# A two-level Winograd matmul: other homes for some results, and a new order of preparatory work in its first three groups

## The chip, the cores and the metric

The kernel runs on one NeuronCore of a Trainium2 chip. The metric is the device time of one execution in microseconds (us), lower is better. A core has a matrix engine (PE), a vector engine (DVE), a scalar engine (ACT), a general engine (POOL), a queue processor (SP) which here issues nearly all transfers, and 16 DMA engines that carry them out. Each engine takes its instructions strictly in the order in which the program gave them, and waits on semaphores for the others.

## The reference

```python
def setup_inputs():
    B, S, D = 8, 2048, 2048
    return {"x": np.random.randn(B, S, D).astype(np.float32),
            "w": np.random.randn(D, D).astype(np.float32)}

def reference(x, w):
    cs = np.cumsum(x, axis=1)
    diff = cs - np.concatenate([np.zeros(...), cs[:, :-1, :]], axis=1)
    return np.matmul(diff, w).astype(np.float32)
```

The differences of a running sum are the terms themselves, so the result is x times w: 16384 rows of x, each of 2048 numbers, times a 2048 x 2048 matrix.

## The kernel before, in words

**Tiles of x.** The 16384 rows are cut into 128 tiles of 128 rows, here called tile 0 to tile 127. The first four are multiplied plainly in bf16 while w still arrives. The others go in groups of four, named by their first tile g: tiles g, g+1, h = g+2 and h+1. Group 4 is done by `group_plain`, groups 8, 12, 16 and so on, by `group`. The change touches the end of the plain part and groups 4, 8 and 12.

**Preparing a tile.** Five steps: `load` (two transfers of 512 KB), `weigh` (ACT sums the absolute values of each half, two instructions, line 112), `scale_of` (two tiny DVE instructions and one on POOL), `narrow` (ACT writes the scaled tile as f16, two instructions, line 143), `turn` (two transposes by DMA, line 156). All tiles share five buffers `F`, so a load has to wait for the tile that had its buffer. Tile 5 is the exception: it is loaded over `xP`, the plain part's turned x, once that part's rows 0 and 1 are done.

**First level.** Two tiles are one block row each of a 2 x 2 block scheme: tile g gives A11 and A12, tile g+1 gives A21 and A22 (halves of its 2048 numbers). w gives B11, B12, B21 and B22, each 1024 x 1024. In Winograd's form seven products take the place of eight, with S1 = A21+A22, S2 = S1-A11, S3 = A11-A21, S4 = A12-S2, and T1 = B12-B11, T2 = B22-T1, T3 = B22-B12, T4 = B21-T2. S1g is the S1 of tiles g and g+1, S1h that of h and h+1. DVE makes the S (`total`, one instruction each, line 502) and the T (`less`, line 499). One `product` on PE is 16 matmuls (8 steps of k, two halves n of 512 columns) into a pair of PSUM banks. In `group_plain` the four pairs are X (banks 0, 1), Y (2, 3), Z (4, 5) and V (6, 7).

**Second level.** In the groups from 8 on, some of the first-level products are themselves done by seven `quarter` products of four matmuls. The "rows" of this level are tiles g and h, and the quarters of w that it needs (`Inner`: Q1, Q2, Q3, Q4) are made once by `first` (Q1 and Q2), `fourth` (Q4) and `third` (Q3): `in_2` from B21, `in_3` from B22, `in_4` from T4, `in_5` from T1. Each of these is four DVE instructions of 128 x 512 (`first` has eight). `in_2`, `in_4` and `in_5` keep their Q4 in one tile, `flow`, which `keep_flow` copies out to memory (`spill`) and `bring_flow` copies back. In group 8 the order of quarters for A12 B21 on PE is: a11, s1, a12, s2, s4, then half of product S2g T2 (P6g), then s3, the other half of P6g, a22, and then the product S2h T2 (P6h) and a part of S3g T3 (P7g). The next seven are `seven(A3, in_3, ...)`, the last are those of T4 with `in_4`.

**Results.** A result tile C (128 x 512, f32) is begun by ACT from PSUM (`keep`, line 539), added to by DVE (`add`, line 542) and stored by SP (`put`, line 553). The seven tiles `c0` to `c6` go round: a tile that is stored goes to the end of the list `free`, and the next user waits until the store has landed. The results of the plain part go through five tiles `o` (`opool`), through spare tiles of the ring `wb`, and for one row through `F`. One 512-column piece of the plain part, `left_over`, is done as 16 matmuls into bank 2 and copied out by ACT.

**Order.** The order of work on each engine is the order of the program text: `after(...)` chains each instruction behind the one before on its engine. So what stands early in the text, stands ahead in an engine's queue, and an instruction that waits, holds all that is behind it.

Of the kernel before, what the change touches and what calls it, by code (L numbers as in the profile page):

```python
# [10 lines left out]
def kernel(  # L11
# [59 lines left out]
    def bank(i):  # L71
        return psum.tile([P, NB], f32, name=f"b{i}")
# [88 lines left out]
    with tc.tile_pool(name="ring", bufs=7) as ring, tc.tile_pool(  # L161
# [100 lines left out]
        def plain_out(h, r):  # L262
            for n in here(h, r):
                if h == r == 0:
                    c = F[:, 2, ds(n * NB, NB)]
                elif h == 0 or r > 0:
                    c = opool.tile([P, NB], f32, name="o")
                else:
                    c = ring.tile([P, NH], bf16, name="wb").bitcast(f32)
                after("act", lambda: nc.scalar.copy(c, ps[r][n]))  # L270
                done.append((c, ds(r * P, P), ds(h * NH + n * NB, NB)))
# [81 lines left out]
        def block(dst, a, h, k, engine):  # L353
            src = whole[k][:, a, h, :].rearrange("p (n c) -> p n c", c=NB)
            if engine == "dve":
                after(
                    "dve", lambda: nc.vector.tensor_scalar(dst[k], src, uinv, None, MUL)
                )
            else:
                after(  # L360
                    "act", lambda: nc.scalar.activation(dst[k], src, COPY, scale=uinv)  # L361
                )


        def finish_row(r):
            for ko in range(KO - KQ, KO):
                plain(1, r, ko)
            plain_out(1, r)


        def left_over(ps):
            for ko in range(KO):
                after(
                    "pe",
                    lambda: nc.tensor.matmul(
                        ps,
                        xP[:, PLAIN - 1, ko, :],
                        (B11, B21)[ko // KH][ko % KH][:, 1, :],
                        start=(ko == 0),
                        stop=(ko == KO - 1),  # L380
                    ),
                )
            c = opool.tile([P, NB], f32, name="o")
            after("act", lambda: nc.scalar.activation(c, ps, COPY, scale=uw))
            done.append((c, ds((PLAIN - 1) * P, P), ds(NB, NB)))

        for k in range(4):
            block(B11, 0, 0, k, "dve")
# [18 lines left out]
        finish_row(2)  # L407
        for k in range(4, KH):
            block(B21, 1, 0, k, "dve")
        finish_row(3)  # L410
        for k in range(KH):
            block(B12, 0, 1, k, "dve")
        left_over(bank(2))
        for c, rows, columns in done:
            after("sp", lambda: put(c, rows, columns, nc.sync))
        weigh(PLAIN + 1)
        scale_of(PLAIN + 1)
        narrow(PLAIN + 1)
        turn(PLAIN + 1)
        load(PLAIN + 3, 0)  # L420
        load(PLAIN + 3, 1)

# [26 lines left out]
    )  # L449
    inner = inpool.tile([P, 24, NB], f16, name="inner")  # L450
    flow = inpool.tile([P, 4, NB], f16, name="flow")
    spill = [spills.tile([P, 4, NB], f16, name=f"spill{i}") for i in range(4)]
    spare = [inner[:, j, :] for j in range(8, 24)]
    spare += [B12[k][:, n, :] for k in range(KH) for n in range(2)]
    spare += [B22[k][:, 0, :] for k in range(4, 8)]
# [1 line left out]
    S1 = [Part(inner[:, ds(2 * i, 2), :]) for i in range(2)]  # L457
    passing = [Quarter(inner[:, j, :]) for j in range(4, 8)]
    free = [cpool.tile([P, NB], f32, name=f"c{i}") for i in range(7)]

    def pair():
        return [one_c() for _ in range(2)]
# [26 lines left out]
    passed = [flow[:, k, :] for k in range(4)]  # L489

    def keep_flow(i):
        after("sp", lambda: nc.sync.dma_start(spill[i], flow))

    def bring_flow(i):
        after("sp", lambda: nc.sync.dma_start(flow, spill[i]))

    def less(dst, p, q):
        for k in range(len(dst)):
# [59 lines left out]
    def puts(c, t, h):  # L558
        for n in range(2):
            put(c[n], t, 2 * h + n)  # L560
# [26 lines left out]
    def group_plain(g, X, Y, Z, V):  # L587
        h = g + 2
        ug, uh, vg = unit[g], unit[h], unit[g + 1]
        A11g, A12g = parts(g)  # L590
        A11h, A12h = parts(h)
        A21g, A22g = parts(g + 1)
        A21h, A22h = parts(h + 1)
        S1g, S1h = S1
        S2g, S2h, S3g, S3h, S4g, S4h = A11g, A11h, A21g, A21h, A12g, A12h
        load(g + 4, 0)
        load(g + 4, 1)
        product(X, A11g, B11, True)
        for k in range(3):
            block(B22, 1, 1, k, "act")  # L600
        C11g = pair()
        keeps(C11g, X, ug)
        for k in range(3, KH):
            block(B22, 1, 1, k, "act" if k < 6 else "dve")
        product(V, A12g, B21, True)
        product(Y, A11h, B11, True)
        adds(C11g, V, ug)
        puts(C11g, g, 0)
        total(S1g, A21g, A22g, ADD)
        total(S3g, A11g, A21g, SUB)  # L610
        total(S2g, S1g, A11g, SUB)
        less(T2[:4], B22[:4], T1[:4])
        product(Z, A12h, B21, True)
        weigh(h + 1)
        C11h = pair()
        keeps(C11h, Y, uh)
        scale_of(h + 1)
        narrow(h + 1)
        turn(h + 1)
        load(h + 4, 0)  # L620
        less(T2[4:], B22[4:], T1[4:])
        vh = unit[h + 1]
        product(V, S1g, T1, True)
        C22 = pair()
        keeps(C22, V, vg)
        total(S4g, A12g, S2g, SUB)
        product(X, S2g, T2, False)
        C12g = pair()
        keeps(C12g, X, ug)
        less(T3, B22, B12)  # L630
        product(V, S4g, B22, False)
        weigh(g + 4)
        scale_of(g + 4)
        narrow(g + 4)
        load(h + 4, 1)
        turn(g + 4)
        load(g + 5, 0)
        load(g + 5, 1)
        product(X, S3g, T3, False)
        total(S1h, A21h, A22h, ADD)  # L640
        total(S3h, A11h, A21h, SUB)
        total(S2h, S1h, A11h, SUB)
        adds(C11h, Z, uh)
        puts(C11h, h, 0)
        adds(C12g, V, ug)
        puts(C12g, g, 1)
        product(Y, S2h, T2, False)
        C12h = pair()
        keeps(C12h, Y, uh)
        adds(C22, X, vg)  # L650
        puts(C22, g + 1, 1)
        total(S4h, A12h, S2h, SUB)
        product(Z, S1h, T1, True)
        weigh(h + 4)
        less(T4, B21, T2)
        scale_of(h + 4)
        C22 = pair()
        keeps(C22, Z, vh)
        narrow(h + 4)
        weigh(g + 5)  # L660
        product(Y, S3h, T3, False)
        in_2.first()
        in_2.fourth()
        load(h + 5, 0)
        load(h + 5, 1)
        keep_flow(0)
        scale_of(g + 5)
        adds(C22, Y, vh)
        puts(C22, h + 1, 1)
        product(Z, S4h, B22, False)  # L670
        in_2.third()
        adds(C12h, Z, uh)
        puts(C12h, h, 1)
        narrow(g + 5)
        turn(h + 4)
        product(X, A22g, T4, False)
        C21 = pair()
        keeps(C21, X, vg)
        puts(C21, g + 1, 0)
        turn(g + 5)  # L680
        load(g + 8, 0)
        load(g + 8, 1)
        in_3.first()
        in_3.fourth()
        in_3.third()
        product(Y, A22h, T4, False)
        C21 = pair()
        keeps(C21, Y, vh)
        puts(C21, h + 1, 0)
        weigh(h + 5)  # L690
        scale_of(h + 5)
        narrow(h + 5)
        turn(h + 5)


    def group(g, X, Y, q, e, v, w):
# [40 lines left out]
        load(next_k, 0)  # L737
        one()
        two()
        if g > PLAIN + 4:  # L740
            total(S1g, A21g, A22g, ADD)
            total(S3g, A11g, A21g, SUB)
            total(S2g, S1g, A11g, SUB)
# [22 lines left out]
        quarter(e, s4, Q.t22, False)  # L766
        add(C11g[1], e, ug)
        put(C11g[1], g, 1)
        total(S1h, A21h, A22h, ADD)
        total(S3h, A11h, A21h, SUB)  # L770
        scale_of(next_g)
        narrow(next_g)
        total(S2h, S1h, A11h, SUB)
        go(P6g, 2)
        quarter(q, s3, Q.Q3, False)
        add(C11h[1], q, uh)
        put(C11h[1], h, 1)
        weigh(next_h)
        load(next_k, 1)
        total(S4g, A12g, S2g, SUB)  # L780
# [105 lines left out]
            scale_of(next_l)  # L886
        else:
            if g == PLAIN + 4:
                in_4.first()
            one()  # L890
            two()
            weigh(next_k)
# [2 lines left out]
            turn(next_h, [0])  # L895
            scale_of(next_k)
            narrow(next_k)
            if g == PLAIN + 4:
                in_4.fourth()
                keep_flow(2)  # L900
                for k in range(4):
                    after("sp", lambda: nc.sync.dma_start(spill[3][:, k, :], in_3.t21[k]))
                in_4.third()
            else:
                in_5.first()
                in_5.fourth()
                keep_flow(1)
            product((v, w), S1g, T1, True)
            C22g = pair()
            keeps(C22g, (v, w), vg)  # L910
            adds(C12g, (v, w), ug)
            puts(C12g, g, 1)
            load(next_l, 0)
            product((q, e), S1h, T1, True)
            C22h = pair()
            keeps(C22h, (q, e), vh)
# [7 lines left out]
            turn(next_k, [0])  # L924
            adds(C22g, X, vg)
            puts(C22g, g + 1, 1)
            go(P7h, 4)
            adds(C22h, Y, vh)
            puts(C22h, h + 1, 1)
# [77 lines left out]
```

## Time and profile before

| what | value |
|---|---|
| time, three runs | 1500.28, 1501.83, 1503.62 us; median 1501.83 |
| the profiled execution, its own time | 1498.61 us |
| its span, first to last instruction | 1496.8 us |
| PE busy in the span | 1474.5 us (99%) |
| DVE busy | 1283.7 us (86%) |
| ACT busy | 914.4 us (61%) |
| share of the span on the chain that ended last, PE | 90% |
| granted clock of PE, mean | 0.998 |

All times below are in us from the start of the span of the profiled execution. A matmul of 128 x 512 is shown as 379 ns long, but a next one starts every 0.216 us (32 of them take 6.91 us on the chain), so a run of matmuls is shown 0.16 us longer than its share of PE. In an answer of the timeline, the columns are start, length, engine, line and operation, output and inputs, the count of instructions that are merged, and in brackets the idle time before them with what ended it.

### The profile page before, as it was taken

What the parts mean: (1) busy time and instruction counts of PE and PEld (TensorE: products, weight loads), DVE (VectorE), ACT (ScalarE), POOL (GpSimd) and SP (SyncE); (2) the same over time, 40 slices, a digit from 0 to 9 for tenths busy, and PEclk for the clock granted to TensorE, in tenths of its full rate; (3) what the DMA queues carried; (4) which work ended last, traced back from release to release, by engine and by line L of the source; (5) the groups of instructions that cost most, each with busy time, mean ns of one, the idle gap of its engine ahead of it and who ended that gap; (6) DMA issues with size and microseconds to landing.
All of it is one profiled execution on the core that took longest, in us unless ns stands there. A gap on an engine that the chain in (4) does not pass through costs nothing.

```text
span 1496.8 us, 21121 instructions
## 1 busy us (share of the span) xinstructions
PE 1474.5 (99%) x6799; PEld 663.8 (44%) x6799; DVE 1283.7 (86%) x2419; ACT 914.4 (61%) x1301; POOL 69.9 (5%) x136
## 2 busy tenths in 40 slices
PE   8988999999999999999999999999999999999998
PEld 3433444444444444444444444444444444444443
DVE  7987778888888888888888888888888888888887
ACT  5866566656666656666556657556656556666552
POOL 0200000000000000000000000000000000000000
PEclk9999999999999999999999999999999999999999
DMA  9988989999989999989998899999898999898983
GB/s 366 351 225 253 245 228 270 262 270 241 267 255 246 267 268 243 259 247 259 261 272 248 255 241 263 265 274 244 255 239 264 271 258 250 262 235 266 271 204 133
DMA packets 386975, 383.64 MB, mean 256 GB/s; under 512 B 275824, under 2 KB 276336, under 8 KB 386736
## 3 DMA queue, kind: packets, MB, share of 16 engines
q1 hardware_dynamic: 386304, 380.46, 91.9%
q0 software_dynamic: 560, 1.84, 0.3%
q8 instruction: 53, 0.87, 0.2%
q14 instruction: 58, 0.48, 0.1%
HBM read 180.88 MB, written 136.31 MB: 212 GB/s over the span
## 4 chain that ended last, share of the span: by engine, by line
PE 90%; DMA 4%; DVE 3%; ACT 2%; issue 1%; SPq 1%; DVEq 0%; ACTq 0%
PE b L531 46%; PE b L512 42%; PE b L250 2%; DVE c L542 2%; DMA W<-in_w_dram 2%; DMA x<-F 1%; DVE W L499 0%; ACT W L361 0%; ACT waste L112 0%; DMA W<-in_x_dram 0%; DMA out_dram<-c 0%; SPq L156 0%; DMA out_dram<-o 0%; DMA F<-in_x_dram 0%; ACT o L270 0%
## 5 line engine op out<-in xcount | busy, mean ns | idle before, releaser
L542 DVE SCALAR_TENSOR_TENSOR c<-b,u,c 128x512 f32<-128x512 f32 x1048 | 744.6, 746 | 164.3 <-PE b L531 92.1
L512 PE MATMUL b<-W,x 128*128 128x512 f16 x3072 | 717.1, 379 | 4.6 <-ACT c L539 2.6
L539 ACT ACTIVATE c<-b,u 128x512 f32<-128x512 f32 x496 | 316.9, 681 | 343.9 <-PE b L531 170.1
L512 PEld LDWEIGHTS <-x 128*128 128x128 f16 x3072 | 300.7, 98 | 369.0 <-issue 6.6
L143 ACT ACTIVATE F<-F,s 128x1024 f16<-128x1024 f32 x246 | 282.3, 1148 | 116.3 <-DVE s L131 112.0
L531 PE MATMUL b<-W,inner 128*128 128x512 f16 x1392 | 338.3, 379 | 0.0
L112 ACT ACTIVATE waste<-F 128x1024 uint8<-128x1024 f32 x246 | 259.6, 1055 | 91.4 <-DMA F<-in_x_dram 87.3
L531 PEld LDWEIGHTS <-inner 128*128 128x128 f16 x1744 | 170.6, 98 | 206.2 <-issue 0.5
L531 PEld LDWEIGHTS <-x 128*128 128x128 f16 x1560 | 152.5, 98 | 194.8 <-issue 15.4
L531 PE MATMUL b<-W,x 128*128 128x512 f16 x968 | 234.3, 379 | 1.4
L502 DVE TENSOR_TENSOR x<-x,x 128x1024 f16<-128x1024 f16 (+1 forms) x214 | 120.4, 574 | 6.5 <-PE b L512 1.1
L132 POOL TENSOR_SCALAR u<-m,uw 128x1 f32<-128x1 f32 x124 | 64.5, 525 | 1314.6 <-DVE m L129 1307.0
L531 PE MATMUL b<-flow,x 128*128 128x512 f16 x352 | 91.2, 382 | 3.1 <-DVE c L542 3.1
L502 DVE TENSOR_TENSOR inner<-x,x 128x1024 f16<-128x1024 f16 (+1 forms) x122 | 67.4, 553 | 3.8 <-DMA x<-F 3.8
L531 PE MATMUL b<-inner 128*128 128x512 f16 x240 | 61.6, 379 | 0.3 <-DVE c L542 0.3
L250 PE MATMUL b<-wb,xP 128*128 128x512 bf16 x240 | 57.4, 393 | 4.3 <-ACT wb L234 3.0
L531 PE MATMUL b<-inner,x 128*128 128x512 f16 x240 | 61.6, 379 | 0.0
L112 ACT ACTIVATION_READ_ACCUMULATOR waste<-F 128x1 f32 x246 | 46.7, 190 | 0.0
L502 DVE TENSOR_TENSOR x<-inner,x 128x1024 f16<-128x1024 f16 x62 | 42.3, 683 | 3.2
L502 DVE TENSOR_TENSOR inner<-inner 128x512 f16<-128x512 f16 x112 | 42.3, 419 | 1.0
L499 DVE TENSOR_TENSOR flow<-W,inner 128x512 f16<-128x512 f16 x120 | 42.6, 416 | 0.0
L237 DVE TENSOR_REDUCE wmax<-W 128x1 f32<-128x1024 f32 x32 | 39.0, 1219 | 3.0 <-DMA W<-in_w_dram 1.4
(54 smaller groups left out, 410.8 us busy)
## 6 DMA issues: line engine op xcount, KB each, us to landing
out_dram<-c SPq DMA_DIRECT2D x496, 256.0 KB, 4.0
F<-in_x_dram SPq DMA_DIRECT2D x246, 512.0 KB, 5.1
flow<-spill SPq DMA_DIRECT2D x57, 512.0 KB, 4.5
W<-in_w_dram SPq DMA_DIRECT2D x32, 512.0 KB, 9.7
W<-in_x_dram SPq DMA_DIRECT2D x16, 256.0 KB, 7.1
x<-F SPq DMA_TRANSPOSE x246, 4.0
out_dram<-o SPq DMA_DIRECT2D x7, 256.0 KB, 3.7
spill<-flow SPq DMA_DIRECT2D x3, 512.0 KB, 2.6
```

The lines of the kernel that those rows point to most:

```text
L112: lambda: nc.scalar.activation(waste, where[t][i], ABS, scale=1.0 / ROW, accum_out=sums_of[t][:, i : i + 1],),
L132: after("pool", lambda: nc.gpsimd.tensor_scalar(u, m, uw, None, MUL))
L143: lambda: nc.scalar.activation(narrowed(t)[:, ds(i * NH, NH)], where[t][i], COPY, scale=s),
L237: lambda: nc.vector.tensor_reduce(wmax[:, i : i + 1], wt, AX.X, MAX, apply_absolute_value=True),
L250: lambda: nc.tensor.matmul(ps[r][n], xP[:, r, ko, :], wb[h, ko][:, ds(n * NB, NB)], start=(ko == 0), stop=(ko == KO - 1),),
L499: after("dve", lambda: nc.vector.tensor_tensor(dst[k], p[k], q[k], SUB))
L502: after("dve", lambda: nc.vector.tensor_tensor(dst.all, p.all, q.all, op))
L512: said = nc.tensor.matmul(to[n], a[k], b[k][:, n, :], start=(first and k == 0), stop=(k == KH - 1), skip_group_check=True,)
L531: said = nc.tensor.matmul(to, a[k], b[k], start=(first and k == 0), stop=(k == 3), skip_group_check=True)
L539: after("act", lambda: nc.scalar.activation(c, p, COPY, scale=u))
L542: after("dve", lambda: nc.vector.scalar_tensor_tensor(c, p, u, c, MUL, ADD))
```

## The change

Eight edits, in the order of the program:

1. `plain_out`: of the plain part's second half, the first piece of row 1 goes to a ring tile and no longer to an `o` tile.
2. `left_over`: its result goes to a buffer of turned x (`turned_x[3][0]`, that of tile 7) in place of an `o` tile, and its store is issued with it; the whole call stands behind `weigh`, `scale_of`, `narrow` and `turn` of tile 5.
3. `weigh` of tile 5 stands ahead of the last row's matmuls and copies (`finish_row(3)`).
4. Group 4: the pair C11h lives in a part of `inner` which is not used until later (the home of `in_3`'s Q1), so the list `free` has two more to give; the list starts one further round.
5. The copies `spill0` and `spill3`, which nothing reads back, are gone: one transfer of 512 KB in group 4 and four of 128 KB in group 8.
6. Group 4's end: `weigh`, `scale_of`, `narrow` and `turn` of tile 11 stand ahead of the `keep` and `put` of the last pair C21; of `in_3`, only Q1 and Q2 are made there, the one ahead of `scale_of` of tile 11 and the other behind it. Its Q4 moves into group 8 behind the sums of x, and its Q3 to where `in_4.first` stood.
7. Group 8: S1h, S3h and S2h stand behind the addition of the quarter s3, and no longer ahead of it.
8. Groups 8 and 12: `first`, `fourth` and `third` of `in_4` (`first` and `fourth` of `in_5`) and the `keep_flow` are spread among and behind the additions of the products with T1.

```diff
@@ plain_out
-                elif h == 0 or r > 0:
+                elif h == 0 or r > 1 or r == 1 and n:
                     c = opool.tile([P, NB], f32, name="o")
                 else:
                     c = ring.tile([P, NH], bf16, name="wb").bitcast(f32)
@@ left_over
-            c = opool.tile([P, NB], f32, name="o")
+            c = turned_x[3][0].rearrange("p k m -> p (k m)").bitcast(f32)
             after("act", lambda: nc.scalar.activation(c, ps, COPY, scale=uw))
-            done.append((c, ds((PLAIN - 1) * P, P), ds(NB, NB)))
+            rows = ds((PLAIN - 1) * P, P)
+            after("sp", lambda: put(c, rows, ds(NB, NB), nc.sync))
...
+        weigh(PLAIN + 1)
         finish_row(3)
         for k in range(KH):
             block(B12, 0, 1, k, "dve")
-        left_over(bank(2))
         for c, rows, columns in done:
             after("sp", lambda: put(c, rows, columns, nc.sync))
-        weigh(PLAIN + 1)
         scale_of(PLAIN + 1)
         narrow(PLAIN + 1)
         turn(PLAIN + 1)
+        left_over(bank(2))
         load(PLAIN + 3, 0)
...
+    free.append(free.pop(0))
@@ group_plain
-        C11h = pair()
+        C11h = [inner[:, ds(j, 2), :].rearrange("p a n -> p (a n)").bitcast(f32) for j in (16, 18)]
         keeps(C11h, Y, uh)
...
         puts(C11h, h, 0)
+        del free[-2:]
...
-        keep_flow(0)
...
-        in_3.first()
-        in_3.fourth()
-        in_3.third()
         product(Y, A22h, T4, False)
+        weigh(h + 5)
+        less(in_3.Q1, in_3.t12, in_3.t11)
+        scale_of(h + 5)
+        narrow(h + 5)
+        less(in_3.Q2, in_3.t22, in_3.Q1)
+        turn(h + 5)
         C21 = pair()
         keeps(C21, Y, vh)
         puts(C21, h + 1, 0)
-        weigh(h + 5)
-        scale_of(h + 5)
-        narrow(h + 5)
-        turn(h + 5)
@@ group
         one()
         two()
+        if g == PLAIN + 4:
+            in_3.fourth()
...
-        total(S1h, A21h, A22h, ADD)
-        total(S3h, A11h, A21h, SUB)
+        if g > PLAIN + 4:
+            total(S1h, A21h, A22h, ADD)
+            total(S3h, A11h, A21h, SUB)
         scale_of(next_g)
         narrow(next_g)
-        total(S2h, S1h, A11h, SUB)
+        if g > PLAIN + 4:
+            total(S2h, S1h, A11h, SUB)
         go(P6g, 2)
         quarter(q, s3, Q.Q3, False)
         add(C11h[1], q, uh)
         put(C11h[1], h, 1)
+        if g == PLAIN + 4:
+            total(S1h, A21h, A22h, ADD)
+            total(S3h, A11h, A21h, SUB)
+            total(S2h, S1h, A11h, SUB)
...
             if g == PLAIN + 4:
-                in_4.first()
+                in_3.third()
...
-            if g == PLAIN + 4:
-                in_4.fourth()
-                keep_flow(2)
-                for k in range(4):
-                    after("sp", lambda: nc.sync.dma_start(spill[3][:, k, :], in_3.t21[k]))
-                in_4.third()
-            else:
-                in_5.first()
-                in_5.fourth()
-                keep_flow(1)
+            Q = in_4 if g == PLAIN + 4 else in_5
+            Q.first()
             product((v, w), S1g, T1, True)
...
             load(next_l, 0)
+            Q.fourth()
+            keep_flow(2 if g == PLAIN + 4 else 1)
             product((q, e), S1h, T1, True)
...
             puts(C22g, g + 1, 1)
+            if g == PLAIN + 4:
+                in_4.third()
             go(P7h, 4)
```

More of the change, by code (lines that the diff above doesn't have):

```diff
@@ L451 @@
     flow = inpool.tile([P, 4, NB], f16, name="flow")
-    spill = [spills.tile([P, 4, NB], f16, name=f"spill{i}") for i in range(4)]
+    spill = [spills.tile([P, 4, NB], f16, name=f"spill{i}") for i in range(1, 3)]
     spare = [inner[:, j, :] for j in range(8, 24)]
@@ L491, in keep_flow @@
     def keep_flow(i):
-        after("sp", lambda: nc.sync.dma_start(spill[i], flow))
+        after("sp", lambda: nc.sync.dma_start(spill[i - 1], flow))
     def bring_flow(i):
-        after("sp", lambda: nc.sync.dma_start(flow, spill[i]))
+        after("sp", lambda: nc.sync.dma_start(flow, spill[i - 1]))
     def less(dst, p, q):
```

## The prediction

> **What bounds the kernel now.** First the page: PE is busy for 99% of the span, so the ceiling on a gain from order alone is the 22 us in which it is not.
>
> ```profile
> span 1496.8 us, 21121 instructions
> PE 1474.5 (99%) x6799; PEld 663.8 (44%) x6799; DVE 1283.7 (86%) x2419; ACT 914.4 (61%) x1301; POOL 69.9 (5%) x136
> ```
>
> Then the windows, to see where PE idles (columns: stretch, length, busy us of PE, PEld, DVE, ACT, POOL, granted clock, DMA share, GB/s). From 270 on a group of 45 us loses nothing; the losses lie in the stretches that the change edits. In 140 to 160 the clock also falls.
>
> ```profile
> 80.00:100.00 20.00, 17.31 (x79) 7.66 (x79) 16.23 (x30) 19.17 (x26) 2.72 (x2) 1.00 0.70 209
> 110.00:120.00 10.00, 7.89 (x37) 3.48 (x36) 7.48 (x16) 5.06 (x9) 0.83 (x1) 1.00 0.89 328
> 140.00:150.00 10.00, 6.89 (x30) 2.76 (x28) 7.34 (x13) 4.61 (x7) 0.77 (x1) 0.94 1.03 265
> 150.00:160.00 10.00, 10.00 (x42) 4.26 (x41) 8.63 (x20) 8.85 (x14) 0.83 (x1) 0.89 1.05 287
> 315.00:360.00 45.00, 44.95 (x209) 20.29 (x208) 39.20 (x76) 27.73 (x40) 1.92 (x4) 1.00 0.92 255
> ```
>
> Last the timeline, for each loss with what ended it. Six waits of PE stand there, in brackets: 1.50, 1.85, 0.44, 2.11, 0.56 and 2.56.
>
> ```profile
> 80.40 10.09 PE L512 MATMUL b<-W,x 128*128 128x512 f16 x46 [1.50 <-ACT o L270]
> 92.34 3.61 PE L512 MATMUL b<-W,inner 128*128 128x512 f16 x16 [1.85 <-DVE inner L502]
> 99.89 10.67 PE L512 MATMUL b<-W,x 128*128 128x512 f16 x48 [0.44 <-ACT c L539]
> 116.34 13.97 PE L512 MATMUL b<-W,x 128*128 128x512 f16 x64 [2.11 <-ACT c L539]
> 141.88 1.90 PE L512 MATMUL b<-W,x 128*128 128x512 f16 x8 [0.56 <-DVE x L502]
> 148.92 1.87 PE L531 MATMUL b<-flow,x 128*128 128x512 f16 x4 [2.56 <-DVE c L542]
> 150.59 5.29 PE L512 MATMUL b<-W,x 128*128 128x512 f16 x20
> ```
>
> And what the engines behind these waits were themselves waiting for:
>
> ```profile
> 79.77 0.59 ACT L270 COPY o<-b 128x512 f32<-128x512 f32 x1 [5.62 <-DMA out_dram<-o]
> 83.52 0.21 DVE L129 TENSOR_SCALAR m<-m 128x1 f32<-128x1 f32 x1 [5.62 <-ACT waste L112]
> 115.60 0.69 ACT L539 ACTIVATE c<-b,u 128x512 f32<-128x512 f32 x1 [4.53 <-DMA out_dram<-c]
> 145.88 0.69 DVE L502 TENSOR_TENSOR inner<-x,x 128x1024 f16<-128x1024 f16 x1 [1.89 <-DMA x<-F]
> ```
>
> So there is no shortage of a resource: a copy waits for a store of its tile, all behind it on ACT waits too, and DVE sits on a sum of tile 11 with an addition behind it that PE wants.
>
> **Part by part.** PE's instructions, their count and order stay; only waits move. From X at 74.86 to the product after the first `seven(A3)` at 163.06, PE spends 88.2 us on 352 matmuls of 0.216, that is 76.0: 12.2 us are lost. The six waits are 9.0, 0.16 us each (1.0) for the overlap of a matmul's tail that a wait breaks, and the clock: the four matmuls at 148.92 take 1.87 where others take 1.02, the 20 behind them 5.29 where those at 197.63 take 4.48, together 1.66. The small rest stays.
>
> *Edits 1, 2 and 3, the plain part's end.* Now the last row needs no sixth `o` tile, so the copy at 79.77 loses its store. But the weighing of tile 5 (2.3 us on ACT) now stands ahead of that row's two copies (0.52 each). Its tile is loaded at 68.15 and takes 6.3 to land (the transfers' view), so 74.45. ACT is free at 73.65, weighs to 76.8, copies to 77.3 and 77.85. PE wants V's banks after X, at 74.86 + 16 x 0.216 = 78.3: the 1.50 goes, with 0.5 to spare; a load later by more than that costs its lateness.
>
> DVE's m of tile 5 comes when the blocks before it end, at 77.90, not 83.52; POOL's one instruction goes with it and nobody waits for it. Narrowing then runs 78.4 to 80.7, the left-over's copy 80.6 to 81.3. Its bank 2 is wanted by the third product Y at 81.8 (0.5 to spare; unhidden it costs up to 0.7). SP turns tile 5 at 79.5 to 82.1, stores the left-over (ready at 81.3, so no wait; 0.45 of issue) and loads tile 7 at 82.7, not 87.85. ACT's blocks of B22 start at 81.2, not 86.20: from here ACT and DVE are **5.0 earlier**. S1g ends at 87.0; its transposes (3.4 to land) are there at 84.3; PE wants it after 64 matmuls, at 88.7. The 1.85 goes. The keeps that end at 100.4 end at 95.4, and PE wants V again at 95.6: the 0.44 goes, with 0.2 to spare.
>
> *Edit 4.* C12h's second tile waited 4.53 for the store of C11h's first. With nine tiles it gets c1, stored long before: ACT keeps at 106.0 to 107.3, PE wants Y at 109.4, the 2.11 goes. Late next is C22h's second: it gets c5, C12g's first, whose store went out at 111.10 and now goes at 106.25; such stores took 5.5 to 5.9, so it lands about 111.9, the keep ends 112.5, and PE wants Z at 112.85. I cost it at nothing, at most 0.7. C11h's new home is written again at 121, ten us after its store.
>
> *Edit 5.* 512 KB leave at 123 (0.33 of SP), another 512 KB at 166 (2.25 of SP). PE waited for neither: nothing, and up to 2 us of DMA slack per piece at the page's 256 GB/s.
>
> *Edit 6.* PE now ends group 4 at 123.2 (130.14 before). Weighing, scaling and narrowing tile 11 runs on ACT from 121.1 to 126.15, and the two keeps of C21 (1.25) behind it end at 126.75 and 127.35. PE wants Y for group 8 at 126.65: **a new wait of 0.6**, from nothing (if the load of tile 11 were earlier still, which doesn't help: ACT is bound by tile 9's narrowing) to 1.3 (if the 0.7 above comes on top). Two stores on SP (1.7) wait behind the two transposes (2.7); the tiles have no taker for 10 us. In exchange tile 11's transposes go out at 129.45, right behind tile 12's loads. Those at 138.73 took 6.1; these have 512 KB of stores less ahead, so land by 137. Q4 of `in_3` (1.42 of DVE) falls into DVE's wait for the first quarter (128.0 to 131.6): nothing.
>
> *Edit 7.* The wait of 0.56 for S2g shrinks to 0.3, since C11h's keeps no longer come late. The addition that PE waited 2.56 for now has no transposes ahead of it: done at 138.65, wanted at 139.6. **2.56 and its tail go, and the clock's 1.66 with it.** Late next is S2h: three sums of 0.7 end at 140.7, PE wants it at 140.45: 0.3 new, and one us more for each us that tile 11 lands after 138.6.
>
> *The clock.* The idle rows of 1.50 to 2.11 left the clock at 1.00, that of 2.56 brought 0.89. The Trainium skill (TensorE: Matmul & The Clock Gate, Part 1) has the clock fall after an idle window of about 3.4 us, free-running, and warns of gaps above that; by this rule a gap of 2.56 would be harmless, the 1.66 not its price, and the gain 8.6. The row is taken.
>
> *Edit 8.* In group 8 DVE has 2.84 more to do than before (Q4 and Q3 of `in_3`, each 1.42, come over from group 4), but `in_3.third` replaces the 2.75 of `in_4.first` ahead of A3's sums, and stall and sums shift together: the seven start with the same lead of DVE (1.0) as now. Behind them T4's Q3 comes before C22h's additions, which end 0.8 later against PE; PE wants that bank 2 us later still. SP's `keep_flow` and its wait come behind two stores and a load, which gain 0.5. Nothing; bound -0.8 (group 16's two waits of 0.26 and 0.58 go too) to +0.8.
>
> **Sum.** Waits that go: 1.50 + 1.85 + 0.44 + 2.11 + 2.56 = 8.46; 0.26 of S2g's; five tails of 0.16 = 0.8; clock 1.66: 11.2. New: 0.6 + 0.3 = 0.9. Gain 10.3. Against the profiled execution 1498.61 this makes 1488.3; that one lay 3.2 below the median, so I forecast 1501.83 - 10.3 = **1491.5**.
>
> **Rivals.** *A: tile 11 stays late.* For it: DMA is at 1.03 of its share from 130 to 150, and group 16 still waits for transposes (0.80 and 0.96 on DVE). Against: it is issued 2 us earlier against PE. Then 2.56, its tail and the clock stay in another place (S2h): gain 10.3 - 4.4 = 5.9, 1495.9.
>
> *B: all small new waits vanish, and group 16's.* Gain 10.3 + 0.9 + 0.8 = 12.0: 1489.8.
>
> *C: no net change.* PE comes 10 us earlier to groups whose tiles are limited by DMA (0.92 to 1.05 of its share from 120 on), and gives the gain back in groups 8 to 16. Against: the steady groups run at the same share without a wait, the five us from 78 to 83 in which DMA moved almost nothing are filled, and 1 MB of stores is gone. 1501.8.
>
> *D, the other side: slower.* The same queue, worse: each of groups 8, 12 and 16 waits for a transposed tile at its first sums. A wait of w costs w + 0.16, and 1.66 of clock from 2.56 on. To be slower by 0.2% it has to eat 10.3 + 3.0, or 4.4 per group: w = 2.6 in each of the three is the point. The waits now are 1.89, 0.20 and 0.96. At w = 4 it costs 17.5 and ends at 1509.
>
> **How the numbers follow.** A change within 0.2%, 3.0 us, can't be told from none. My case 55%, A 18%, B 13%, C 6%, D 8%. My case, A and B are faster: 0.86; C same: 0.06; D slower: 0.08. My case's own range, with the bounds 0.7 and 0.7 and 0.8 up, 1.5 down, and a run-to-run spread of 1.7: 1488.5 to 1495. The range reaches to B below and A above with that spread: 1487.5 to 1498.5, which leaves out C and D.
>
> **What would show it.** Right: no bracket on the second product's wait for line 270; the vector engine's m of tile 5 near 78; no ACT wait on a store before Y's third use; tile 11's transposes ahead of C21's stores; no clock below 1.00 between 100 and 200; `seven` 10 us earlier, the steady groups 45.1 as before. Wrong: ACT idle before tile 5's weighing (load late); a bracket over 0.7 on PE for Z; DVE waiting for x<-F in group 8 by more than 1 us, or groups 12 and 16 longer than 46.3.

## The result, and the profile after

The changed kernel takes 1495.08 us (median of 12 runs, 1492.38 to 1498.42), the kernel before 1501.5 us in the same comparison (12 runs, 1498.82 to 1504.58). The ratio is 0.9959, with a 95% interval of 0.9948 to 0.9969: faster by 0.41%, some 6.2 us. The forecast was 1491.5 with 10.3 us of gain. The direction was right, the size too large by 4 us.

The profiled execution of the changed kernel took 1496.11 us, its span is 1494.3. Page, changed kernel:

```profile
span 1494.3 us, 21105 instructions
...
PE 1473.4 (99%) x6793; PEld 663.4 (44%) x6799; DVE 1283.9 (86%) x2419; ACT 913.6 (61%) x1301; POOL 69.4 (5%) x136
```

The engines' work is the same: the weight loads of PE and the instructions of DVE, ACT and POOL have the counts of before (six matmul records are missing from this trace). The timeline of PE, changed kernel, with every wait between the plain part's end and group 16 (columns as before; lines 512, 531, 539 and 542 of the kernel before are 514, 533, 541 and 544 here):

```profile
72.59 3.62 PE L375 MATMUL b<-W,xP 128*128 128x512 f16 x16
...
89.86 3.62 PE L514 MATMUL b<-W,inner 128*128 128x512 f16 x16
...
98.15 0.38 PE L514 MATMUL b<-W,x 128*128 128x512 f16 x1 [0.44 <-ACT c L541]
98.73 10.30 PE L514 MATMUL b<-W,x 128*128 128x512 f16 x47 [0.20 <-ACT c L541]
...
117.33 13.76 PE L514 MATMUL b<-W,x 128*128 128x512 f16 x63 [1.18 <-ACT c L541]
131.48 0.38 PE L514 MATMUL b<-W,x 128*128 128x512 f16 x1 [0.40 <-ACT c L541]
132.06 3.40 PE L514 MATMUL b<-W,x 128*128 128x512 f16 x15 [0.20 <-ACT c L541]
...
140.18 1.90 PE L514 MATMUL b<-W,x 128*128 128x512 f16 x8 [0.40 <-DVE x L504]
...
145.84 3.63 PE L514 MATMUL b<-W,x 128*128 128x512 f16 x16 [0.31 <-DVE x L504]
150.33 0.38 PE L514 MATMUL b<-W,x 128*128 128x512 f16 x1 [0.86 <-ACT c L541]
150.91 0.81 PE L514 MATMUL b<-W,x 128*128 128x512 f16 x3 [0.20 <-ACT c L541]
...
156.38 1.02 PE L533 MATMUL b<-W,x 128*128 128x512 f16 x4 [0.29 <-DVE c L544]
...
159.11 7.07 PE L514 MATMUL b<-W,inner 128*128 128x512 f16 x32
...
234.45 1.02 PE L533 MATMUL b<-inner 128*128 128x512 f16 x4 [1.11 <-DVE c L544]
241.38 1.02 PE L533 MATMUL b<-flow,x 128*128 128x512 f16 x4 [0.73 <-DVE c L544]
```

The large waits of before (1.50, 1.85, 2.11, 2.56) are gone, and nothing waits for line 270. In their place stand smaller ones, most of them on an ACT `keep`. What ACT itself waited for (timeline of ACT, changed kernel):

```profile
91.66 1.06 ACT L112 ACTIVATE waste<-F 128x1024 uint8<-128x1024 f32 x1 [1.94 <-DMA F<-in_x_dram]
116.59 0.69 ACT L541 ACTIVATE c<-b,u 128x512 f32<-128x512 f32 x1 [3.55 <-DMA out_dram<-c]
147.06 1.06 ACT L112 ACTIVATE waste<-F 128x1024 uint8<-128x1024 f32 x1 [2.08 <-DMA F<-in_x_dram]
```

Three transfers come too late: tile 7's load, the store of C12g's first tile, tile 14's load. Behind each of them a `keep` is queued whose PSUM bank PE wants. The windows of the changed kernel show the clock whole, and the steady group as it was (44.95 of 45 busy):

```profile
140.00:160.00 20.00, 18.16 (x81) 7.76 (x82) 15.13 (x31) 12.42 (x18) 1.11 (x2) 1.00 1.08 269
315.00:360.00 45.00, 44.95 (x209) 20.35 (x208) 39.20 (x76) 27.86 (x40) 1.92 (x4) 1.00 0.99 257
```

**One number for the stretch.** All of the change acts between the left-over's first matmul (line 375) and the product behind the first `seven(A3)` (the row of 32 matmuls, at 159.11 here). In between lie 368 matmuls, 79.5 us at 0.216. I call the time between these two rows the stretch: 162.89 - 71.41 = 91.48 before, 159.11 - 72.59 = 86.52 after. The two rows of the kernel before:

```profile
71.41 3.62 PE L375 MATMUL b<-W,xP 128*128 128x512 f16 x16
...
162.89 7.07 PE L512 MATMUL b<-W,inner 128*128 128x512 f16 x32
```

The stretch is read from each kernel's PE timeline, and leaves out the plain part, whose loads of w vary by a microsecond from run to run (line 375 starts between 70.92 and 72.75 in these profiles).

### The profile page after: what moved, and what is told of

Its sections match the earlier page's. It is cut to its first block, busy times and chain, and to the rows that moved or that the text cites. A ratio compares the mean times of both kernels' runs of the same rounds, so it can differ in the third digit from the quotient of the medians.

```text
span 1494.3 us, 21105 instructions
## 1 busy us (share of the span) xinstructions
PE 1473.4 (99%) x6793; PEld 663.4 (44%) x6799; DVE 1283.9 (86%) x2419; ACT 913.6 (61%) x1301; POOL 69.4 (5%) x136
## 3 DMA queue, kind: packets, MB, share of 16 engines
q0 software_dynamic: 560, 1.84, 0.3%
## 4 chain that ended last, share of the span: by engine, by line
PE 88%; DMA 5%; DVE 3%; ACT 2%; issue 1%; SPq 1%; DVEq 0%; ACTq 0%
PE b L533 45%; PE b L514 41%; DVE c L544 2%; PE b L250 2%; DMA W<-in_w_dram 2%; DMA F<-in_x_dram 2%; DMA x<-F 1%; DVE W L501 1%; ACT waste L112 0%; DMA W<-in_x_dram 0%; DMA out_dram<-wb 0%; ACT F L143 0%; SPq L156 0%; DVE x L504 0%; ACT wb L234 0%
## 5 line engine op out<-in xcount | busy, mean ns | idle before, releaser
L234 ACT CAST wb<-W 128x1024 bf16<-128x1024 f32 x32 | 32.2, 1059 | 15.6 <-DMA W<-in_w_dram 12.3
```

The source lines that it names most:

```text
L234: after("act", lambda: nc.scalar.copy(b, wt))
```

## The experiments

Two theories stood against each other. W: each wait has its own price, and the gain fell short because ACT runs into the three late transfers. D: the DMA engines are the bound in these groups, so PE gives back later whatever it wins. The column "stretch" is from one profile of each kernel (two of the kernel before and of the changed one). Each ratio is to the kernel before in the same comparison, and a difference between two rows of the table has an interval of about 0.0016 either way, 2.4 us: of the kernels built on the changed one, only the last two rows differ from it by more than that. For the others, the medians and the stretch have to be read together.

| kernel | median, us | ratio to before, 95% interval | stretch, us | group 16's waits |
|---|---|---|---|---|
| before (two profiles) | 1501.5 | | 91.48, 94.22 | 0.84, 1.00 |
| changed (two profiles) | 1495.08 | 0.9959 (0.9948 to 0.9969) | 86.52, 87.17 | 1.84, 2.13 |
| edits 1 to 3 alone | 1498.07 | 0.9977 (0.9967 to 0.9986) | 89.39 | 1.43 |
| edit 7 alone | 1500.33 | 0.9993 (0.9984 to 1.0002) | 92.37 | 1.19 |
| edit 4 alone | 1498.78 | 0.9978 (0.9969 to 0.9987) | 90.94 | 0.96 |
| changed, edit 7 undone | 1494.42 | 0.9951 (0.9939 to 0.9964) | 86.31 | 1.81 |
| changed, tile 11 behind again | 1494.77 | 0.9955 (0.9942 to 0.9969) | 85.81 | 2.29 |
| changed, tile 7's load early | 1495.85 | 0.9968 (0.9956 to 0.9981) | 85.57 | 1.98 |
| changed, home for C12g | 1492.95 | 0.9948 (0.9935 to 0.9960) | 83.79 | 2.78 |
| changed, tile 14's weighing behind | 1492.75 | 0.9945 (0.9932 to 0.9957) | 84.67 | 1.87 |
| these three together | 1491.48 | 0.9940 (0.9926 to 0.9954) | 82.56 | 1.63 |
| the last two of the three | 1492.59 | 0.9936 (0.9924 to 0.9949) | 82.05 | 1.45 |

### Edits 1 to 3 alone

The kernel before with the first three hunks of the change (`plain_out`, `left_over` and the place of tile 5's weighing).

> The kernel before with edits 1 to 3 alone (the plain part's end). Theory W (each wait has its own price; the changed kernel falls short of the forecast because ACT runs into three transfers that land too late: tile 7's load, the store of c5, tile 14's load): the waits of 1.50 and 1.85 go with their tails, the third (0.44) grows to some 1.7 us because tile 7's load lands after ACT wants it; gain about 2.5 us. C12h's store wait and the 2.56 with the fallen clock stay, at about the same size. Theory D (the DMA engines are the bound in these groups, so PE gives back later whatever it wins): PE starts group 8 earlier, but the waits in group 8 and at Y for C12h grow by as much; gain 0 to 1 us.

Measured: 0.9977, 3.2 us by the medians. PE's first two waits are gone, and the third, at V, is split in two as in the changed kernel (0.31 and 0.20): the 80 matmuls from 89.18 to 107.28 lost 0.8, where W had expected some 1.7. C12h's wait for its store stayed, and was larger than in the first profile of before: 3.63, with the clock down. W's gain of 2.5 lies in the interval (2.1 to 5.0 us); D's 0 to 1 doesn't. The wait in group 8 is 1.57 here, though, not 2.56.

### Edit 7 alone

```diff
-        total(S1h, A21h, A22h, ADD)
-        total(S3h, A11h, A21h, SUB)
+        if g > PLAIN + 4:
+            total(S1h, A21h, A22h, ADD)
+            total(S3h, A11h, A21h, SUB)
         scale_of(next_g)
         narrow(next_g)
-        total(S2h, S1h, A11h, SUB)
+        if g > PLAIN + 4:
+            total(S2h, S1h, A11h, SUB)
         go(P6g, 2)
         quarter(q, s3, Q.Q3, False)
         add(C11h[1], q, uh)
         put(C11h[1], h, 1)
+        if g == PLAIN + 4:
+            total(S1h, A21h, A22h, ADD)
+            total(S3h, A11h, A21h, SUB)
+            total(S2h, S1h, A11h, SUB)
```

> The kernel before with edit 7 alone (S1h, S3h, S2h of group 8 behind the addition). Theory W: the wait of 2.56 before the quarter a22 goes, the clock stays at 1.00 (1.66 more), and S2h, which still waits for tile 11's transposes that land near 145.8, holds the next product by about 0.9 us; gain 3 to 3.7 us. Theory D: the same transposes hold PE elsewhere for the same time; gain 0 to 1 us, and the clock falls all the same.

Measured: 0.9993, with an interval that holds 1, and 1.0 us by the medians. W's 3 to 3.7 is out. D's 0 to 1 holds, and the clock fell all the same, as D had said; but the place is not the one that D gave, as the timeline of PE for this kernel shows:

```profile
119.04 23.34 PE L512 MATMUL b<-W,x 128*128 128x512 f16 x95 [3.63 <-ACT c L539]
147.10 1.90 PE L512 MATMUL b<-W,x 128*128 128x512 f16 x8 [0.41 <-DVE x L502]
152.76 4.49 PE L512 MATMUL b<-W,x 128*128 128x512 f16 x20 [0.31 <-DVE x L502]
```

In its own place the edit does all that was forecast: the wait before the quarter a22 is gone, 0.31 before S2h's product remains, and the clock is at 1.00 there. But the wait at 119 is 3.63, not 2.11, and 95 matmuls took 23.34, of which 20.5 are their share at full clock. That wait lies ahead of the edit, in code that is the same as before. So it had to vary by itself, which the second profile of the kernel before was to tell.

### Edit 4 alone

```diff
+    free.append(free.pop(0))
...
-        C11h = pair()
+        C11h = [inner[:, ds(j, 2), :].rearrange("p a n -> p (a n)").bitcast(f32) for j in (16, 18)]
...
         puts(C11h, h, 0)
+        del free[-2:]
```

> The kernel before with edit 4 alone (C11h in inner, the list one round further). Theory W: the wait of 2.11 for C12h's second tile goes, and C22h's second, which now needs the store of C12g's first, is wanted near 118.4 while the store lands near 117, so no new wait; gain about 2.2 us, unless the 2.56 in group 8 grows with it, since tile 11's transposes are bound to the ACT chain. Theory D: gain 0 to 0.5 us, all given back at the wait for tile 11's transposes.

Measured: 0.9978, 2.5 us by the medians: W's 2.2 is met, D's 0 to 0.5 is not. The wait for C12h's tile is gone, but C22h's second tile came late as in the changed kernel (PE 0.88 at 120.75), which was not expected here. In the same profile PE waited 2.24 at 93.63, before the product of S1g, and the granted clock from 90 to 100 was 0.83; a wait of 2.24 again, at 149.65, left it at 1.00. Timeline of PE, this kernel:

```profile
93.63 5.30 PE L513 MATMUL b<-W,inner 128*128 128x512 f16 x16 [2.24 <-DMA F<-in_x_dram]
...
149.65 1.02 PE L532 MATMUL b<-flow,x 128*128 128x512 f16 x4 [2.24 <-DVE c L543]
```

### The kernel before, a second profile

No edit.

> The kernel before, unchanged, for a second profile. If the waits on a store vary from run to run: C12h's wait for its tile is anywhere from 4.5 to 6.5 us on ACT, PE's wait at Y 2.1 to 3.7, and where it is over 3 the clock falls there and not in group 8, whose wait is then about 1.6. If they don't vary: 2.1 and 2.56 again, with the clock at 0.89 from 150 to 160.

Timeline of PE, the kernel before, second profile:

```profile
80.26 10.09 PE L512 MATMUL b<-W,x 128*128 128x512 f16 x46 [1.84 <-ACT o L270]
92.54 3.61 PE L512 MATMUL b<-W,inner 128*128 128x512 f16 x16 [2.19 <-DVE inner L502]
118.23 22.35 PE L512 MATMUL b<-W,x 128*128 128x512 f16 x95 [3.79 <-ACT c L539]
151.72 1.02 PE L531 MATMUL b<-flow,x 128*128 128x512 f16 x4 [1.93 <-DVE c L542]
```

The waits on transfers do vary. The store of C11h's first tile took 6.70 from issue to landing in place of 5.39; ACT waited 6.21 for it in place of 4.53, and PE 3.79 in place of 2.11. The clock fell there, to 0.88 from 120 to 130, and in group 8 it was whole, with a wait of 1.93. So the profile on which the forecast's sum was made was a good one: its stretch was 2.7 us shorter than this one's. And the two waits go together: where the first was over 3.6 (here, and with edit 7 or edits 1 to 3 alone), the clock fell there, and the wait in group 8, where the code still had it, was 1.6 to 1.9. So edit 7 alone had a wait of 1.6 to 1.9 to take away, without a fall of the clock, and not the 4.4 of the first profile. The 1 us that it brought fits that; one profile of it can't show more.

### The changed kernel without edit 7

> The changed kernel with edit 7 undone (the sums S1h, S3h, S2h ahead of the addition again). Theory W: tile 11 is earlier in the changed kernel, so the quarter a22 waits for three sums, 0.7 to 1.5 us, without a fall of the clock; S2h's wait of 0.31 behind it goes; 0.5 to 1.2 us slower than the changed kernel, so 5 to 6 us faster than before. Rival: edit 7 carries most of the gain; the 2.56 and the fallen clock come back, and the kernel is 4 us slower than the changed one, 2 to 3 us faster than before.

Measured: 0.9951, against 0.9959 with the edit: no difference. Its stretch is 86.31. Timeline of PE, this kernel:

```profile
145.01 1.02 PE L533 MATMUL b<-flow,x 128*128 128x512 f16 x4 [1.40 <-DVE c L544]
```

Before the quarter a22 PE waits 1.40, because DVE waits 0.72 for tile 11's transposes, and the addition that PE wants stands behind the sums made from them. So with edit 6 and without edit 7 most of the wait is still there: with neither edit in this part it is 1.57 (edits 1 to 3 alone) and 2.24 (edit 4 alone). It costs nothing here, because in exchange the 0.31 before S2h's product and the 0.86 before P7g are gone (0.20 of the latter is left). Both theories had given it a cost.

### The changed kernel with tile 11 behind again

```diff
-        weigh(h + 5)
         less(in_3.Q1, in_3.t12, in_3.t11)
-        scale_of(h + 5)
-        narrow(h + 5)
         less(in_3.Q2, in_3.t22, in_3.Q1)
-        turn(h + 5)
         C21 = pair()
         keeps(C21, Y, vh)
         puts(C21, h + 1, 0)
+        weigh(h + 5)
+        scale_of(h + 5)
+        narrow(h + 5)
+        turn(h + 5)
```

> The changed kernel with one piece of edit 6 undone: weighing, scaling, narrowing and turning tile 11 stand behind the keeps and stores of the last C21 again; the rest of the change stays. Theory P (place decides: edit 6 brings tile 11 early enough that PE's 2.56 and the clock go even without edit 7): DVE's sum S1h waits 2 to 3 us for tile 11's transposes, PE waits 1.5 to 2.5 before the product of S2h (0.31 now), Y's 0.40 and 0.20 go; 0.5 to 2 us slower than the changed kernel. Rival (edit 7 alone cures that wait): no wait over 0.5 before the product of S2h, 0.5 us faster than the changed kernel.

Measured: 0.9955 and a stretch of 85.81, the same as with it. PE waits 0.78 before S2h's product in place of 0.31, and the 0.40 and 0.20 for C21h's keeps are gone. DVE waits 0.38 for tile 11, not 2 to 3. My expectation was wrong: tile 11's transposes, issued at 136.06 here, land early enough. So edit 7 cures the wait before a22 without this piece of edit 6. Of the two edits that I credited with the largest term, each can be taken out alone without a loss in time; what the changed kernel would take without both was not run.

### Tile 7's load early

```diff
+        load(PLAIN + 3, 0)
+        load(PLAIN + 3, 1)
         for c, rows, columns in done:
             after("sp", lambda: put(c, rows, columns, nc.sync))
...
         left_over(bank(2))
-        load(PLAIN + 3, 0)
-        load(PLAIN + 3, 1)
```

> The changed kernel, with tile 7's two loads issued ahead of the plain part's stores in place of behind the left-over's store. Theory W: tile 7 has landed when ACT wants to weigh it, ACT's waits of 1.94 and 0.19 go, and PE no longer waits for C22's keeps (0.44 and 0.20, some 1.7 us with what they hold up); 1 to 1.7 us faster than the changed kernel. Theory D: the same megabyte only moves, the stores and tile 8 come later for it, and the wait turns up at the next transfer (Z for C22h, or group 8); 0 to 0.4 us.

Measured: 0.9968, not faster than the changed kernel. In its place it worked: ACT no longer waits for tile 7, both brackets at V are gone, and the stretch is 0.95 to 1.6 us shorter than in the two profiles of the changed kernel. Tile 5's transposes went out 1.5 us later against the left-over (83.68 with line 375 at 72.75; 82.05 with 72.59), and DVE waited 1.42 for them: one megabyte ahead pushes back what stands behind, as D has it. PE shows no bracket there in this kernel, and group 16's waits are as large as before. So the profile has a gain that the five times don't show; whether it is lost further on or hidden in the spread, these runs don't tell.

### A home for C12g

```diff
-        C12g = pair()
+        C12g = [inner[:, ds(j, 2), :].rearrange("p a n -> p (a n)").bitcast(f32) for j in (20, 22)]
...
         puts(C12g, g, 1)
+        del free[-2:]
```

> The changed kernel, with the pair C12g also in a part of inner that is unused until the end of group 4 (the home of in_3's Q2), so no result waits for a store in group 4. Theory W: ACT's wait of 3.55 for the store goes, and PE's 1.18 at Z with it (about 1.5 us with its tail); narrowing tiles 10, 9 and 11 comes some 3 us earlier, so the wait of Y for C21h's keeps (0.40 and 0.20) shrinks too; 1.3 to 2.2 us faster than the changed kernel. Theory D: the loads and transposes behind it come no earlier, DVE waits for them in group 8; 0 to 0.5 us.

Measured: 0.9948, 2.1 us by the medians faster than the changed kernel; stretch 2.7 to 3.4 shorter. No result of group 4 waits for a store, the bracket of 1.18 is gone, and the one for C21h's keeps shrank to 0.20. W's 1.3 to 2.2 is met by the medians and passed by the stretch. By the ratio alone (0.9948 against 0.9959, with overlapping intervals) D's 0 to 0.5 would not be out.

### Tile 14's weighing behind the keeps

```diff
-        weigh(next_h)
+        if g > PLAIN + 4:
+            weigh(next_h)
...
         C12g = pair()
         keeps(C12g, X, ug)
+        if g == PLAIN + 4:
+            weigh(next_h)
...
-        scale_of(next_h)
-        narrow(next_h)
-        load(next_l, 1)
+        if g > PLAIN + 4:
+            scale_of(next_h)
+            narrow(next_h)
+            load(next_l, 1)
...
             one()
             two()
+            if g == PLAIN + 4:
+                scale_of(next_h)
+                narrow(next_h)
+                load(next_l, 1)
             weigh(next_k)
```

> The changed kernel, with the weighing of tile 14 in group 8 behind the keeps of C12g, and its scale and narrowing behind the sums for the next seven quarters. Theory W: the keeps no longer stand behind ACT's waits of 2.08 and 0.35 for the load, PE's 0.86 and 0.20 before P7g go; about 1.2 us faster than the changed kernel. Theory D: tile 14 is narrowed and turned 2 us later, and group 12 waits for it; 0 us or slower.

Measured: 0.9945, 2.3 us by the medians; stretch 1.9 to 2.5 shorter. Timeline of PE, this kernel:

```profile
145.45 4.49 PE L514 MATMUL b<-W,x 128*128 128x512 f16 x20 [0.31 <-DVE x L504]
156.97 7.07 PE L514 MATMUL b<-W,inner 128*128 128x512 f16 x32
```

P6h and the first part of P7g now run as one row of 20. The bracket of 0.29 at 156.38 is gone too. ACT still comes to a load that hasn't landed (it waits 0.57 and 0.18 for it), but nothing that PE wants stands behind it: the wait was one of order, and D's give-back in group 12 did not come. W had expected 1.2.

### The three together, and the last two alone

> The changed kernel with the three edits of the three runs before together. Theory W: the gains add, 3.5 to 5 us faster than the changed kernel, 10 to 11 us faster than before, which is the size that was forecast for the change. Theory D: under 1.5 us, because a part of it turns up as DVE waits for transposes in groups 8 to 16.

Measured: 0.9940, 10.1 us by the medians faster than before, 3.6 faster than the changed kernel; stretch 82.56, 3 us above its matmuls. That is the size that had been forecast for the change itself. Timeline of PE, the three together, all brackets up to group 16:

```profile
90.39 3.61 PE L514 MATMUL b<-W,inner 128*128 128x512 f16 x16 [0.73 <-PE b L514]
129.49 3.40 PE L514 MATMUL b<-W,x 128*128 128x512 f16 x15 [0.20 <-ACT c L541]
137.61 1.90 PE L514 MATMUL b<-W,x 128*128 128x512 f16 x8 [0.41 <-DVE x L504]
143.27 4.49 PE L514 MATMUL b<-W,x 128*128 128x512 f16 x20 [0.31 <-DVE x L504]
...
230.66 1.02 PE L533 MATMUL b<-inner 128*128 128x512 f16 x4 [1.63 <-DVE c L544]
```

> The changed kernel with the new home of C12g and tile 14's weighing behind the keeps, tile 7's loads left where they are. If the three gains simply add: 1.0 us slower than with all three. If the early loads of tile 7 only push back tile 5's transposes, and with them S1g and the transfers behind, as PE's 0.73 there suggests: the same time within 0.5 us, about 1491.5.

Measured without the early load of tile 7: 0.9936, against 0.9940 with it; the medians say 1.1 us the other way. The two can't be told apart, and the stretch is 0.5 longer with the early load (82.56 against 82.05). Both beat the changed kernel.

### The changed kernel, a second profile

No edit.

> The changed kernel, unchanged, for a second profile. If the shortfall is one of place and not of chance: the same three ACT waits for transfers (tile 7's load, about 2 us; C12g's store, about 3.5; tile 14's load, about 2), each within 1 us, and PE's waits behind them.

The three ACT waits are there again: 1.89 for tile 7, 3.60 at C22h's second tile (the view puts it down to a DVE instruction, which doesn't touch that tile; that it is the store again is inferred), 2.23 and 0.78 for tile 14. Behind them stand PE's brackets: 0.44 and 0.20, 1.23, and 1.52 with 0.20. They belong to the kernel, not to one run. ACT also waited 3.23 for tile 12's load, where 1.58 and 1.30 stood in the first profile; no PE bracket hangs on it.

## Why the prediction was right or wrong

**The bound, and where the losses lay: right.** The steady groups did not change (45.1 each, as before). All of the gain that the profiles show arose in the stretch, 91.48 to 86.52 in the first profile of each, 5 us; by the means of two profiles each 92.85 to 86.85, 6 us.

**Edits 1 to 3: right in their first half.** Tile 5 was weighed at 74.74 and the last row's copies ended at 78.0, PE met no wait at V; DVE's m of tile 5 came at 79.00 (77.90 plus this run's later start of 1.2); S1g was ready in time. The step that failed is "the 0.44 goes, with 0.2 to spare". The forecast issued tile 7's load at 82.7 and gave its landing no price. It went out at 85.71, 1.8 us later even with the shift of 1.2: SP's eight stores took 6.1 us (75.40 to 81.5), so that tile 5's transposes went out at 82.05, where 79.5 and the shift were counted; the two took 2.9. Its two halves then took a median of 6.4 us to land, where the first of these loads took 4.2 before and the next two a median of 6.0. Cost: the 80 matmuls from 89.86 to 108.87 should take 17.27 and took 19.01, so 1.74.

**Edit 4: mechanism right, a term mis-sized.** "At nothing, at most 0.7" was the price of C12g's store. It cost 1.18 and the tail of 0.16, 1.34: that store went out later than forecast, at 109.83, and took 6.7 to land, not the 5.5 to 5.9 of the one profile. The second profile of the kernel before has 6.7 for such stores too: the range of that row could not be had from one profile.

**Edit 5: nothing seen against it**, and not tried alone.

**Edit 6: the new wait is there**, 0.40 and 0.20 with two tails, 0.9, forecast 0.6.

**Edit 7: the wait and the fallen clock are gone, as forecast; the reason was too narrow.** S2g's 0.40 and S2h's 0.31 stand where 0.3 and 0.3 were forecast, without their tails. But the 4.4 us of it (2.56, tail, clock) was not its usual price: with the longer store wait ahead of it, it is 1.6 to 1.9 and the clock's fall belongs to the other wait. And the changed kernel lost no time without edit 7, where 1.40 of the wait came back, nor without the earlier tile 11 of edit 6.

**A step that was missing: P7g.** The forecast had tile 14's load without a word. ACT waited 2.08 and 0.35 for it with C12g's keeps behind, and PE lost 0.86 and 0.20 with two tails, 1.38, and 0.3 more at the quarter at 156.38, whose addition stood behind the next keeps. Moving that weighing took all of it away and gained 2.3 us by the medians.

**Edit 8 and group 16: the bound of 0.8 was too tight.** Edit 8 was not tried alone. Group 16's two waits rose, in sum, from 0.84 and 1.00 in the two profiles of the kernel before to 1.84 and 2.13 in those of the changed one: about 1 us is given back there. DVE waits for transposes of x in both kernels. Why they come later is not settled: the DMA share from 220 to 245 is 1.10 in the changed kernel and 1.09 before, so a fuller queue doesn't show; without edit 8 the sum was already 1.43 with edits 1 to 3 alone; and no run took away a transfer there.

**Sum.** Forecast 10.3. Not foreseen: 1.74 + 1.34 + 1.38 + 0.3 = 4.8 in the stretch, 0.6 of tails in the forecast's own new waits (0.3 at Y, 0.16 each at S2g and S2h), about 1 in group 16. That leaves 3.9; the profile on which the sum was made was some 1.4 us better in the stretch than the mean of the two, which makes 5.3, against the 6.2 measured. So two errors ran against each other: terms that were missing, and a kernel before that usually loses more than in its first profile.

**The rivals.** A (tile 11 stays late) is out: DVE waited for tile 11's transposes in neither profile of the changed kernel. Its 1495.9 is still the forecast nearest to the time measured, by chance: other waits made up the same sum. B is out. C and D said that DMA gives the gain back. As the main cause they are refuted by the two edits that cured a wait in its place and, together, kept their gain to the end (0.9936). Pieces of them are true: the early load of tile 7 showed no gain in the time, and group 16 gave back 1 us. One argument against C was misread: from 78 to 83 the DMA engines of the kernel before were busy for 0.90 of the time at 316 GB/s; the quiet stretch is from 83 to 86 (a share of 0.02 and less). The range held because A's end reached up to 1498.5, so by luck; my case's own range, 1488.5 to 1495, missed by 0.1.

**The signs named ahead.** Of the right ones, most came: no wait for line 270, m of tile 5 at 79.00 (later by the shift), no wait on a store before Y's third use, tile 11's transposes (134.37) ahead of C21's stores (140.39), the clock whole, the steady groups at 45.1. But the seven started at 151.55 against 155.71 before, 4 us earlier and not 10. Of the wrong ones three came: 1.18 on PE for Z; 1.31 us in which DVE waited for tile 10's transposes in group 8, which cost PE nothing; and group 16, 47.25 long (223.69 to 270.94), over the 46.3.

**The clock.** The rule that was weighed, a gap of about 3.4 us (the Trainium skill, TensorE: Matmul & The Clock Gate, Part 1), would have let 2.56 pass. Here the clock fell with waits of 2.24, 2.56, 3.63 (twice) and 3.79, and stayed whole with 1.85, 2.11, 2.19 and also with another 2.24. So a bare threshold on the gap doesn't fit, neither theirs nor mine. Nor is a fall's price fixed: 1.7 us behind the 2.24, the 2.56, the 3.79 and one 3.63, and 2.7 behind the other 3.63 (edit 7 alone). The page's own remark that the window runs freely would allow the two cases of 2.24 to differ, but no run here shows the window itself.

## What to carry to other kernels

When a change takes away a wait, every instruction behind it comes earlier, and each of them that needs a transfer has to be given the transfer's landing time as a price: the three largest terms that were missed or too small here were ACT instructions that met a load or a store which the earlier waits had hidden. Where such an instruction holds a `keep` or copy that frees a PSUM bank, put the copy ahead of it; that order alone brought some 2 us here (medians 2.3, stretch 1.9 to 2.5), with ACT still waiting for the load. A margin of 0.2 or 0.3 us against a transfer is no margin if the same transfer takes 5.4 us in one profile and 6.7 in the next: take a second profile of the unchanged kernel before trusting a sum of waits.

## What was not expected of the hardware

The same 256 KB store, in the same code, took 5.39 us from issue to landing in one profile and 6.70 in another, and, since ACT needed that tile again at once, this moved PE by 1.7 us and brought a fall of the clock of about as much again: the 95 matmuls behind the wait of 3.79 took 22.35 where 95 at full clock, tail included, take 20.7. And SP's issue of a store is no constant: a median of 0.55 us for the six from 110.11 in the kernel before, 0.76 on average for the eight at the plain part's end in the changed one.
